# A streaming-encoder layer: the order of feed-forward pieces and block products behind the first part

## The chip, the core and the metric

The kernel runs on one core of a Trainium2 chip. The time is that of one execution on the device, in microseconds; before the change it is 1093.76 us, the median of three runs (1093.75 to 1093.88). Weights and activations are float32. TensorE (PE) multiplies, ScalarE (ACT) and VectorE (DVE) prepare its operands and work on its results, SyncE (SP) and GpSimd (POOL) issue transfers.

## What is computed

One layer: attention in two groups of heads, then a feed-forward with a causal convolution. The change touches the feed-forward alone:

```python
def conv_ffn(h, w_up_l, conv_w_l, conv_b_l, w_down_l):
    u = h @ w_up_l                                   # 256 x 2048 @ 2048 x 11264
    u = causal depthwise convolution of width 3 (u) + conv_b_l
    gate, val = jnp.split(u, 2, axis=-1)             # 5632 features each
    return (jax.nn.silu(gate) * val) @ w_down_l      # @ 5632 x 2048
```

There are 256 tokens, 2048 model columns and 5632 hidden features: 44 feature tiles of 128.

## The kernel before

**High and low.** A float32 weight tile `w_raw` is split in two: `w_hi` is a cast by ACT to the format that PE multiplies (L263), and `w_lo = w_raw - w_hi` is a subtraction by DVE (L271). PE multiplies `w_hi` with both parts of the activations (512 columns: high and low side by side) and `w_lo` with their high part alone (256 columns). `w_hi` and `w_lo` have three buffers each, taken in turn, `w_raw` has five. So the cast for one step takes the buffer of the step three before it, and waits until PE has done that step's products with `w_hi`.

**Parts and pieces.** The 44 feature tiles are cut into five parts of eight tiles and a last part of four (`FFN_PARTS`). Inside a part the tiles go in pairs; a pair is done for the gate and then for the value. The products of a pair with `w_up` need 16 blocks of rows, in two pieces of eight (`up_pieces`, `kh` 0 and 1), each one step: 16 products with `w_hi`, 16 with `w_lo`, all into one accumulator `pu`. A part of eight tiles has 16 such steps. When a pair's second piece is done, `convolved` brings the result through the convolution: ACT copies one half (L1061), DVE adds and scales (L1062, L1064), ACT makes the three taps (L1071, L1078), DVE adds them (L1083). The gate goes through SiLU on ACT (L1089); the value is multiplied with it by DVE (L1097) and split again into high and low, `g2` (L1100, L1102). After the last pair of a part, DVE and ACT also make sums of its tiles (L1111 to L1125), called `s`.

**Block products.** The multiplication with `w_down` works on the part before: `down_in_seven` computes a 2 x 2 block product with seven products of four blocks, one step each, with 8 products with `w_hi` and 4 with `w_lo`, all 512 columns wide. Their weights are loaded, or made by adding: a DVE sum of two raw tiles (L1233), or a transfer by POOL that adds into a raw tile (L1206). DVE adds each result to the output rows `xb` (L1175). A part has 14 such steps, for two halves of the output columns; they are dealt out among the up steps of the next part. The last part of four tiles has seven among its 8 up steps, and seven more after them, mixed with the plain pieces of its own `w_down` product (`down_plain`, accumulator `acc`).

**What sets the order.** All steps stand in one list. For each step in turn the kernel issues: what follows from earlier steps (the stages of `convolved`, in turn), the cast and subtraction for the step two ahead (`SPLIT`), the load for the step six ahead (`LOAD`), the DVE sum for the step four ahead (`SUM`), and the products of the step itself. PE, DVE, ACT and SP keep this order; each is a queue in which an instruction that waits holds up all behind it.

In part 0, which has no block products among its pieces, the second piece of a pair (but the last pair) does its products with `w_lo` first: `lows` is (1, 0) there, so that low follows low and high follows high between the pieces.

Of the kernel before, what the change touches and what calls it, by code (L numbers as in the profile page):

```python
# [45 lines left out]
def hybrid_layer(  # L46
# [173 lines left out]
    steps, following, after, waiting, running, others = [], [], [], deque(), [], []  # L220
# [5 lines left out]
    def new_step(load, sums, prepare, matmuls, follow=None, first=False):  # L226
        steps.append((load, sums, prepare, matmuls, follow, first))
# [12 lines left out]
    def acc_tile(name):  # L240
        nonlocal psa
        if psa is None:
            psu_ctx.close()
            psa = ctx.enter_context(
                tc.tile_pool(name="psa", bufs=1, space=bass.MemoryType.PSUM, side="right", reuse_waits="tile")
            )
        turn[0] ^= 1
        return psa.tile([P, 2, 512], F32, name=name, tag=f"acc{turn[0]}")
# [4 lines left out]
    def load(src, raw=None):  # L253
        if raw is None:
            raw = wraw.tile([P, 2048], F32, name="w_raw", tag="w_raw")
        a, b = src.shape[1:]
        nc.sync.dma_start(raw[:, : a * b].rearrange("p (a b) -> p a b", a=a), src)
        return raw
# [7 lines left out]
    def split(raw, a, b):  # L266
        return subtracted(raw, *cast(raw, a * b, act.copy), a, b)
# [9 lines left out]
    def rows_of(w, k0, n, c0, cols):  # L277
        return w[k0 * P : (k0 + n) * P, c0 : c0 + cols].rearrange("(k p) c -> p k c", p=P)
# [848 lines left out]
    def up_pieces(part, f0, follows):  # L1127

        c0 = f0 * P + (DFF if follows is val_follows else 0)
        cell, at_step = [], []  # L1130

        def piece(kh):
            mem = {}
            at_step.append(len(steps))
            lows = (1, 0) if kh and part.f_lo == 0 and f0 < part.f_hi - 2 and at_step[1] == at_step[0] + 1 else (0, 1)

            def loads():
                mem["raw"] = load(rows_of(wu, 8 * kh, 8, c0, 2 * P))

            def prepare():  # L1140
                mem["parts"] = split(mem["raw"], 8, 2 * P)

            def matmuls():
                if kh == 0:
                    cell.append(acc_tile("pu"))
                acc, (hi, lo) = cell[0], mem["parts"]
                first = kh and part.f_lo == f0 == 0 and follows is gate_follows
                halves = (range(4), range(4, 8)) if first else (range(8),)
                order = (0, 1) if first else lows
                for ks, low, j in [(ks, low, j) for ks in halves for low in order for j in range(2)]:  # L1150
                        for i in ks:
                            k = 8 * kh + i
                            nc.tensor.matmul(  # L1153
                                acc[:, j, S:] if low else acc[:, j, :],
                                (lo if low else hi)[:, i, j * P : (j + 1) * P],
                                hT[:, k, 0, :] if low else hT[:, k].rearrange("p a b -> p (a b)"),
                                start=k == 0 and not low, stop=k == KT - 1 and low == order[1],
                            )

            new_step(loads, None, prepare, matmuls, (lambda: follows(part, cell[0], f0)) if kh else None)  # L1160

        piece(0)
        yield
        piece(1)
        yield

# [122 lines left out]
    for f_lo, f_hi in FFN_PARTS:  # L1289
        part = Part(f_lo, f_hi)  # L1290
        pieces = [
            p for f in range(f_lo, f_hi, 2) for follows in (gate_follows, val_follows)
            for p in [up_pieces(part, f, follows)] * 2
        ]
        if last is None:
            behind = []
        elif f_hi < NFT:
            behind = [g for c in (0, 1024) for g in [down_in_seven(last, c)] * 7]
        else:
            second = down_in_seven(last, 1024)  # L1300
            behind = [down_in_seven(last, 0)] * 7
        behind = deque(behind)
        at_piece = range(len(pieces) - len(behind), len(pieces))
        for i, piece in enumerate(pieces):
            next(piece)
            if i in at_piece:
                next(behind.popleft())
        if f_hi < NFT:
            last = part
# [109 lines left out]
```

## Time and profile before

| | |
|---|---|
| time, median of three runs | 1093.76 us (1093.75 to 1093.88) |
| profiled execution, first to last instruction | 1091.8 us |
| what the median has around that span | 1.96 us |
| PE busy | 1087.3 us |
| DVE busy | 924.2 us |
| ACT busy | 755.1 us |
| feed-forward, from the first product of its first up step | from 384.2 us on |

The page groups instructions by line, engine and tile; the views used below also list instructions in order of time, as "start, length, engine, line, operation, out<-in, shape, count", with the idle time before and what ended it in brackets. PE's rows overlap a little, since matmuls are pipelined: the distance between the starts of two rows is the time that the first one takes of PE.

### The profile page before, as it was taken

To read this page: it belongs to the slowest core of one execution; us is meant where nothing else is said; L and a number is where in the kernel's file an instruction comes from. 1 tells how busy PE (TensorE), PEld (TensorE's weight loads), DVE (VectorE), ACT (ScalarE), POOL (GpSimd) and SP (SyncE) were. 2 spreads that over 40 slices of the span, in tenths; PEclk is the share of its full clock that TensorE was granted. 3 is DMA by queue.
4 is the path that set the end of the run, shared out by engine and by line. 5 is a ranking of instruction groups with operands and counts; after the bars stand their busy time and mean duration, and the time that the engine had idled before them with its cause. 6 is when DMAs were issued, how large, how long until landed. Compare 5 with 4: busy or idle time off the path is not lost.

```text
span 1091.8 us, 14685 instructions
## 1 busy us (share of the span) xinstructions
PE 1087.3 (100%) x5701; PEld 939.5 (86%) x5701; DVE 924.2 (85%) x918; ACT 755.1 (69%) x968; POOL 59.0 (5%) x53
## 2 busy tenths in 40 slices
PE   9999999999999999999999999999999999999998
PEld 9988888888888888888888888888888888888887
DVE  5988899888897667779887988889898889879996
ACT  6767697767766657767766776677667767667763
POOL 0000000001000000000000000100000000000000
PEclk9999999999999999999999999999999999999999
DMA  8897886868777465669989597996969799896995
GB/s 310 276 272 239 271 206 196 253 183 271 239 214 251 154 199 161 214 170 249 288 206 316 173 265 254 254 296 170 302 195 271 241 246 279 215 319 161 291 247 155
DMA packets 175215, 258.53 MB, mean 237 GB/s; under 512 B 4632, under 2 KB 98218, under 8 KB 175146
## 3 DMA queue, kind: packets, MB, share of 16 engines
q1 hardware_dynamic: 151690, 210.26, 56.9%
q0 software_dynamic: 23280, 47.19, 24.5%
q8 instruction: 45, 0.74, 0.3%
q14 instruction: 24, 0.20, 0.1%
q10 hardware_dynamic: 176, 0.14, 0.0%
HBM read 255.48 MB, written 2.10 MB: 236 GB/s over the span
## 4 chain that ended last, share of the span: by engine, by line
PE 100%; DVE 0%; issue 0%
PE pu L1153 45%; PE bank_a L291 18%; PE bank_b L291 11%; PE bank_c L291 6%; PE acc_o L291 6%; PE acc_v L411 4%; PE bank_e L291 2%; PE acc L291 2%; PE ps_x L192 1%; PE ps_h L637 1%; PE ps_o L709 1%; PE ps_z L785 0%; PE ps_o L710 0%; PE ps_z L805 0%; PE ps_i L186 0%; PE half L291 0%
## 5 line engine op out<-in xcount | busy, mean ns | idle before, releaser
L271 DVE TENSOR_TENSOR w_lo<-w_raw,w_hi 128x2048 fp32r<-128x2048 f32 (+2 forms) x251 | 555.9, 2219 | 124.1 <-ACT w_hi L263 123.1
L263 ACT CAST w_hi<-w_raw 128x2048 fp32r<-128x2048 f32 (+2 forms) x251 | 464.6, 1854 | 220.7 <-PE pu L1153 90.0
L1153 PE MATMUL pu<-hT,w_hi 128*128 128x512 f32 x1408 | 333.6, 390 | 0.0
L1153 PEld LDWEIGHTS pu<-hT,w_hi 128*128 128x128 f32 x1408 | 263.1, 188 | 53.6
L1153 PEld LDWEIGHTS pu<-hT,w_lo 128*128 128x128 f32 x1408 | 180.0, 191 | 6.5
L1153 PE MATMUL pu<-hT,w_lo 128*128 128x256 f32 x1408 | 182.1, 283 | 0.0
L1206 POOL DMA_DIRECT2D w_raw<-in_w_down_dram x31 | 39.8, 1302 | 715.9 <-DVE w_lo L271 384.7
L1078 ACT ACTIVATE tap<-up,ccol 128x256 f32<-128x256 f32 x176 | 74.6, 495 | 0.0
L291 PE MATMUL bank_a<-w_hi,hT 128*128 128x512 f32 x192 | 48.5, 395 | 0.0
L291 PEld LDWEIGHTS bank_a<-w_hi,hT 128*128 128x128 f32 x192 | 35.2, 188 | 6.7
L291 PE MATMUL bank_b<-w_hi,s 128*128 128x512 f32 x160 | 40.1, 393 | 0.0
L291 PE MATMUL bank_a<-w_hi,s 128*128 128x512 f32 x160 | 40.0, 392 | 0.0
L291 PE MATMUL bank_a<-w_hi,g 128*128 128x512 f32 x152 | 38.0, 392 | 0.0
L411 PE MATMUL acc_v<-w_hi,hT 128*128 128x344 f32 x192 | 35.7, 328 | 0.0
L291 PEld LDWEIGHTS bank_b<-w_hi,s 128*128 128x128 f32 x160 | 28.8, 189 | 5.5 <-issue 0.3
L291 PEld LDWEIGHTS bank_a<-w_hi,s 128*128 128x128 f32 x160 | 28.9, 189 | 5.2
L1083 DVE TENSOR_TENSOR gate<-gate,tap 128x512 f32<-128x512 f32 x44 | 30.3, 689 | 2.7 <-DVE gate L1083 0.5
L1083 DVE TENSOR_TENSOR val<-val,tap 128x512 f32<-128x512 f32 x44 | 30.3, 689 | 2.3
L291 PE MATMUL acc_o<-w_hi,oSb 128*128 128x512 f32 x128 | 31.8, 397 | 0.0
L1064 DVE TENSOR_TENSOR up<-t,R 128x512 f32<-128x512 f32 x44 | 30.5, 692 | 1.5
L291 PEld LDWEIGHTS bank_a<-w_hi,g 128*128 128x128 f32 x152 | 27.4, 189 | 4.9
L411 PEld LDWEIGHTS acc_v<-w_hi,hT 128*128 128x128 f32 x192 | 30.4, 190 | 0.5 <-DVE hT L203 0.2
(293 smaller groups left out, 1411.2 us busy)
## 6 DMA issues: line engine op xcount, KB each, us to landing
w_raw<-in_w_up_dram SPq DMA_DIRECT2D x88, 1024.0 KB, 7.0
w_raw<-in_w_down_dram SPq DMA_DIRECT2D x44, 1024.0 KB, 6.7
w_raw<-in_w_in_dram SPq DMA_DIRECT2D x40, 1024.0 KB, 5.5
w_raw<-in_w_down_dram POOLq DMA_DIRECT2D x31, 1024.0 KB, 9.8
w_raw<-in_w_out_dram SPq DMA_DIRECT2D x16, 1024.0 KB, 7.7
w_raw<-in_w_in_dram POOLq DMA_DIRECT2D x10, 1024.0 KB, 9.4
w_raw<-in_w_in_dram SPq DMA_DIRECT2D x13, 516.0 KB, 5.5
xb<-in_x_dram POOLq DMA_DIRECT2D x4, 512.0 KB, 8.7
```

Of the source, the lines that this page charges most:

```text
L192: nc.tensor.transpose(ps[:, j, t * P : (t + 1) * P], x2[:, t, (k + j) * P : (k + j + 1) * P], ident)
L263: copy(hi[:, :n], raw[:, :n])
L271: dve.tensor_tensor(lo[:, :n], raw[:, :n], f32(hi[:, :n]), op=ALU.subtract)
L291: nc.tensor.matmul(o, lhs(i, l, t), r[:, i, :] if cut is None else r[:, i, cut], start=starts and j == 0, stop=stops and j == 3 * n - 1, s ...
L411: nc.tensor.matmul(banks[j][t][:, :VC], of_half(hT[:, k], l, t), w[:, 0, m * VC : (m + 1) * VC], start=k == l == 0 and w is mem["parts", i ...
L637: nc.tensor.transpose(ps[:, h, :], rows[n, t][:, h * HD : (h + 1) * HD], ident)
L709: mm(po, v, w[:, i, :S], start=m == 0, stop=False)
L1064: dve.tensor_tensor(u[:, :, 2:], t2, R, op=ALU.mult)
L1078: act.activation(taps[w][:, j, :], u[:, j, w : w + S], AF.Copy, scale=ccol[:, w, f : f + 1])
L1083: dve.tensor_tensor(a, a, tap, op=ALU.add)
L1153: nc.tensor.matmul(acc[:, j, S:] if low else acc[:, j, :], (lo if low else hi)[:, i, j * P : (j + 1) * P], hT[:, k, 0, :] if low else hT[: ...
L1206: nc.gpsimd.dma_start(mem[weights].rearrange("p (a b) -> p a b", a=4), plus, accum_op=ALU.add)
```

## The change

```diff
@@ up_pieces
-        cell, at_step = [], []
+        cell = []
 
         def piece(kh):
             mem = {}
-            at_step.append(len(steps))
-            lows = (1, 0) if kh and part.f_lo == 0 and f0 < part.f_hi - 2 and at_step[1] == at_step[0] + 1 else (0, 1)
+            lows = (1, 0) if kh and (part.f_lo or f0 < part.f_hi - 2) else (0, 1)
@@ the loop over the parts
         at_piece = range(len(pieces) - len(behind), len(pieces))
         for i, piece in enumerate(pieces):
             next(piece)
-            if i in at_piece:
+            for _ in {i - 1, i}.intersection(at_piece) if i % 2 else ():
                 next(behind.popleft())
```

In every part behind the first, the block products no longer follow each up step but come two at a time behind each pair; the first two pairs of a part are followed by no product and by two, and in the last part by one and by two. The second piece of every pair there now does its products with `w_lo` first. What is multiplied, loaded and added stays the same. Lines below L1134 move up by one.

On PE, where the second group of products of part 1 stands (`pu` is an up step, `bank_b` a block product). Before:

```order
L1153 MATMUL pu<-hT,w_hi 128x512 x16
L1153 MATMUL pu<-hT,w_lo 128x256 x16
L291 MATMUL bank_b<-w_hi,s 128x512 x8
L291 MATMUL bank_b<-w_lo,s 128x512 x4
L1153 MATMUL pu<-hT,w_hi 128x512 x16
L1153 MATMUL pu<-hT,w_lo 128x256 x16
```

Now:

```order
L1152 MATMUL pu<-hT,w_hi 128x512 x16
L1152 MATMUL pu<-hT,w_lo 128x256 x32
L1152 MATMUL pu<-hT,w_hi 128x512 x16
L291 MATMUL bank_b<-w_hi,s 128x512 x8
L291 MATMUL bank_b<-w_lo,s 128x512 x4
```

Two up steps stand in a row, with all 32 products with `w_lo` between those with `w_hi`, and two products (the second has rows like the first) behind them.

On PE, at the start of part 1, with the numbers of the tiles. Before:

```order
L1153 MATMUL pu_4237<-hT_94,w_hi_4131 128x512 x16
L1153 MATMUL pu_4237<-hT_94,w_lo_4132 128x256 x16
L1153 MATMUL pu_4237<-hT_94,w_hi_4177 128x512 x16
L1153 MATMUL pu_4237<-hT_94,w_lo_4178 128x256 x16
L1153 MATMUL pu_4333<-hT_94,w_hi_4226 128x512 x16
```

Now:

```order
L1152 MATMUL pu_4237<-hT_94,w_hi_4131 128x512 x16
L1152 MATMUL pu_4237<-hT_94,w_lo_4132 128x256 x16
L1152 MATMUL pu_4237<-hT_94,w_lo_4178 128x256 x16
L1152 MATMUL pu_4237<-hT_94,w_hi_4177 128x512 x16
L1152 MATMUL pu_4333<-hT_94,w_hi_4226 128x512 x16
```

The part's second up step ends with `w_hi_4177`, where it ended with `w_lo_4178`.

On DVE, at the end of the last part, from the subtraction for the seventh block product on. Before:

```order
L271 TENSOR_TENSOR w_lo<-w_raw,w_hi 128x2048
L1175 TENSOR_TENSOR xb<-xb,bank_a 128x512
L271 TENSOR_TENSOR w_lo<-w_raw,w_hi 128x2048
L1233 TENSOR_TENSOR w_raw<-w_raw 128x2048
L271 TENSOR_TENSOR w_lo<-w_raw,w_hi 128x2048
L1062 TENSOR_TENSOR t_8911<-pu,t_8911 128x512
L1064 TENSOR_TENSOR up_3440<-t_8911,R_90 128x2x256
L1175 TENSOR_TENSOR xb<-xb,bank_a 128x512
L271 TENSOR_TENSOR w_lo<-w_raw,w_hi 128x2048
L1083 TENSOR_TENSOR val<-val,tap 128x512 x2
L1097 TENSOR_TENSOR gate<-gate,val 128x512
```

Now (the first row holds the subtractions for the sixth and seventh product and for the first of the last seven):

```order
L271 TENSOR_TENSOR w_lo<-w_raw,w_hi 128x2048 x3
L1062 TENSOR_TENSOR t_8891<-pu,t_8891 128x512
L1064 TENSOR_TENSOR up_3440<-t_8891,R_90 128x2x256
L1232 TENSOR_TENSOR w_raw<-w_raw 128x2048
L1174 TENSOR_TENSOR xb<-xb,bank_a 128x512
L271 TENSOR_TENSOR w_lo<-w_raw,w_hi 128x2048
L1083 TENSOR_TENSOR val<-val,tap 128x512 x2
L1097 TENSOR_TENSOR gate<-gate,val 128x512
L1174 TENSOR_TENSOR xb<-xb,bank_a 128x512
L271 TENSOR_TENSOR w_lo<-w_raw,w_hi 128x2048
L1102 TENSOR_TENSOR g_8946<-gate,g_8946 128x512
```

The convolution of the last pair (L1062, L1064) and the sum of raw tiles (L1232) now stand ahead of the subtraction for the second of the last seven products, and the taps ahead of the third.

## The prediction

> **What bounds the kernel now.** I read the page first, then the waits, then the order of time on each engine at three places of the feed-forward.
>
> ```profile
> span 1091.8 us, 14685 instructions
> PE 1087.3 (100%) x5701; PEld 939.5 (86%) x5701; DVE 924.2 (85%) x918; ACT 755.1 (69%) x968; POOL 59.0 (5%) x53
> PEclk9999999999999999999999999999999999999999
> PE 100%; DVE 0%; issue 0%
> ACT w_hi L263 <- PE pu L1153: 90.0, 42, 3.0
> ```
>
> PE (TensorE) is busy throughout, the chain that ended last lies on it alone, and its clock was granted in full. So there are two ways to change the time: matmuls that take less room one behind the other, or PE waiting, which it does not do now. VectorE (DVE) has 15% to spare on average, but an average says nothing about one stretch. The last row shows who sets ACT's pace: the cast that makes `w_hi` waits for PE to finish the step three earlier, whose buffer it takes (three buffers of `w_hi`, three of `w_lo`).
>
> Names: U0, U1, ... are the up steps of a part (an odd one is the second piece of its pair), P0 to P6 the seven products put between them, S0 to S6 the last seven products, A0 the first plain piece between S2 and S3. "Highs" are the products with `w_hi`, "lows" those with `w_lo`.
>
> **What the change saves.** Part 0 already runs its pairs as all later ones now shall, so its rows give the price.
>
> ```profile
> 404.49 7.45 PE L1153 MATMUL pu<-hT,w_hi 128*128 128x512 f32 x32
> 448.94 7.44 PE L1153 MATMUL pu<-hT,w_hi 128*128 128x512 f32 x32
> 456.22 2.08 PE L1153 MATMUL pu<-hT,w_lo 128*128 128x256 f32 x16
> 489.62 2.08 PE L1153 MATMUL pu<-hT,w_lo 128*128 128x256 f32 x16
> ```
>
> From 404.49 to 448.94 lie four pairs of the merged form (32 highs, 32 lows): 44.45 / 4 = 11.112 us each. From 456.22 to 489.62 lie six steps in the form high, low, high, low: 33.40 / 6 = 5.567, so 11.133 a pair. A merged pair saves 0.021 us. It holds for 8 pairs in each of parts 1 to 4 and 4 in part 5: 36 x 0.021 = **0.75 us saved**. Two products side by side save nothing beyond that: their matmuls are as wide as the highs.
>
> **What it costs: the buffer that comes free late.** A second piece with its lows first finishes its highs last, so its `w_hi` is released about 1.9 us later than now. And where two products follow a pair, a cast must wait for that pair's end, with 5.4 us of PE work, not 8.3, to cover it and what follows. Three places are tight.
>
> *Start of part 1.* In the new order U1's highs end with the step, at 485.97, and not at 484.06, where its lows begin today.
>
> ```profile
> 484.06 2.08 PE L1153 MATMUL pu<-hT,w_lo 128*128 128x256 f32 x16
> 484.26 1.91 ACT L263 CAST w_hi<-w_raw 128x2048 fp32r<-128x2048 f32 x1 [1.07 <-PE pu L1153]
> 486.23 2.29 DVE L271 TENSOR_TENSOR w_lo<-w_raw,w_hi 128x2048 fp32r<-128x2048 f32 x1 [1.15 <-ACT w_hi L263]
> 485.97 3.82 PE L1153 MATMUL pu<-hT,w_hi 128*128 128x512 f32 x16
> 493.80 2.28 DVE L271 TENSOR_TENSOR w_lo<-w_raw,w_hi 128x2048 fp32r<-128x2048 f32 x1
> 496.00 2.49 DVE L1125 TENSOR_TENSOR s<-gate,s 128x512 fp32r<-128x512 f32 x4
> 496.72 1.09 ACT L1071 ACTIVATE gate<-up,ccol 128x256 f32<-128x256 f32 x2 [2.19 <-DVE s L1125]
> 497.72 1.70 ACT L1078 ACTIVATE tap<-up,ccol 128x256 f32<-128x256 f32 x4
> 499.32 1.90 ACT L263 CAST w_hi<-w_raw 128x2048 fp32r<-128x2048 f32 x1
> 501.25 4.62 DVE L271 TENSOR_TENSOR w_lo<-w_raw,w_hi 128x2048 fp32r<-128x2048 f32 x2 [0.76 <-ACT w_hi L263]
> 502.57 3.79 PE L1153 MATMUL pu<-hT,w_hi 128*128 128x512 f32 x16
> ```
>
> The cast at 484.26 takes U1's buffer. PE to ACT takes 0.2 us (484.06 to 484.26), so it moves to 486.17: 1.91 later. From 486.23 on DVE has no gap until 498.4 (convolution, the sums of products, the four `s`), ACT's `gate` at 496.72 waits for `s`, and the cast at 499.32 stands behind the taps. All of it moves by 1.91: that cast, U4's, ends at 503.13. U4 starts at about 502.55 in both orders (the same steps lie ahead): **0.7 us** of waiting, with 0.1 for the hand-over. Then DVE still has, in a row, the subtraction of U4 (2.2), two operations of the convolution (1.33), an addition (0.6) and U5's subtraction (2.29), from 503.2: it ends at 509.6. U5 starts with its lows, at 503.25 + 5.55 = 508.8: **0.9 us** more.
>
> *Start of parts 2 to 4.* From U3's end, T: U4's cast starts at T + 0.2 at best (U3's buffer) and at T + 0.55 where the taps ahead of it are late, and ends 1.9 later. DVE then does U4's subtraction, 1.33 of convolution, the sum of two raw tiles (2.2, no such step in part 1), an addition and U5's subtraction: 0.55 + 1.97 + 2.2 + 1.33 + 2.2 + 0.6 + 2.29 = 11.1. U5's lows are due at T + 5.44 + 5.55 = 11.0. I take **0.2 us** for each of the three; from none to 0.6, by when the taps end.
>
> *The end of part 5.* Here P5, P6, S0, S1, S2 are five products in a row, 2.72 us each.
>
> ```profile
> 1038.29 1.90 ACT L263 CAST w_hi<-w_raw 128x2048 fp32r<-128x2048 f32 x1
> 1040.70 2.29 DVE L271 TENSOR_TENSOR w_lo<-w_raw,w_hi 128x2048 fp32r<-128x2048 f32 x1
> 1043.02 2.29 DVE L1233 TENSOR_TENSOR w_raw<-w_raw 128x2048 f32<-128x2048 f32 x1
> 1045.23 2.29 DVE L271 TENSOR_TENSOR w_lo<-w_raw,w_hi 128x2048 fp32r<-128x2048 f32 x1
> 1047.43 0.68 DVE L1062 TENSOR_TENSOR t<-pu,t 128x512 f32<-128x512 f32 x1
> 1048.15 0.69 DVE L1064 TENSOR_TENSOR up<-t,R 128x512 f32<-128x512 f32 x1
> 1048.76 0.68 DVE L1175 TENSOR_TENSOR xb<-xb,bank_a 128x512 f32<-128x512 f32 x1
> 1049.35 2.28 DVE L271 TENSOR_TENSOR w_lo<-w_raw,w_hi 128x2048 fp32r<-128x2048 f32 x1
> 1051.56 1.48 DVE L1083 TENSOR_TENSOR val<-val,tap 128x512 f32<-128x512 f32 x2
> 1053.07 0.69 DVE L1097 TENSOR_TENSOR gate<-gate,val 128x512 f32<-128x512 f32 x1
> 1054.28 2.28 DVE L271 TENSOR_TENSOR w_lo<-w_raw,w_hi 128x2048 fp32r<-128x2048 f32 x1
> 1056.48 0.69 DVE L1102 TENSOR_TENSOR g<-gate,g 128x512 fp32r<-128x512 f32 x1
> 1047.02 1.98 PE L291 MATMUL bank_a<-w_hi,g 128*128 128x512 f32 x8
> 1049.74 1.98 PE L291 MATMUL bank_c<-w_hi,g 128*128 128x512 f32 x8
> 1051.56 1.07 PE L291 MATMUL bank_c<-w_lo,g 128*128 128x512 f32 x4
> ```
>
> Today S0's cast runs at 1038.29, before U7 (the last up step) has even started, since it takes P5's buffer. DVE works without a gap from there, and S1's `w_lo` (1045.23 + 2.29 = 1047.52) is ready 4.0 us before its lows at 1051.56; S2's (1051.63) 2.7 us before its own (1049.74 + 2.72 + 1.82 = 1054.28); A0's (1056.56) 0.4 before 1057.0. In the new order S0's cast takes U7's buffer and must wait for X, the end of U7. From X, with steps as the rows are spaced: cast 0.2 + 1.97 = 2.17; S0's subtraction 2.2, t and up 1.33, the sum 2.2, an addition 0.6, S1's subtraction 2.29: 10.8, with the hand-over 10.86. S1's lows are due after P5, P6, S0 and S1's highs: 3 x 2.72 + 1.82 = 9.98. **0.9 us.** Then taps 1.5, product 0.6, addition 0.6, S2's subtraction 2.29: 15.85, due at 10.86 + 0.9 + 1.82 = 13.6. **2.2 us.** Then `g` 0.6, addition 0.6, A0's subtraction 2.29: 19.25, due at 15.85 + 0.9 + 1.82 = 18.55. **0.7 us.** A0 (two products' length, 5.44) gives DVE room again. So 3.8 in all.
>
> **Sum.** 0.7 + 0.9 + 3 x 0.2 + 3.8 = 6.0 us of waiting, less 0.75: **+5.25 us**, a span of 1097.05. The median of the runs (1093.76) lies 1.96 over the profiled span; with the same around it, **1099.0 us**. The hand-over from DVE or ACT to PE is not seen, as PE never waits; from ACT to DVE it is 0.03 us (499.32 + 1.90 to 501.25), from PE to ACT about 0.2. I took 0.07 to 0.1, near the first; with either end the eight waits change by -0.4 to +0.8. At other places the same sums leave room (0.5 us at part 5's U3 and U5, over 2 us in the steady pairs), so they cost nothing while transfers land as now.
>
> The clock was granted in full in all 40 slices, with no gap in PE's work to try it. [...]
>
> **Rivals.**
>
> *Not slower: the waits are hidden.* If U7's late release did not hold S0's cast, or DVE had a store of finished tiles, only the 0.75 us would be left: 1093.0. For it: PE waits nowhere now, and even S1's `w_lo` is 4.0 us early. Against it: that lead is the third buffer, and the late release takes just that; it needs DVE to be 4 us ahead at U7's end, while the rows show it working without a gap to 1057. It decides where S1's subtraction ends under X + 9.98. Chance 0.12.
>
> *The end alone.* The start of part 1 has room that I do not see (DVE in another order of arrival, an earlier `s`), and parts 2 to 4 lose nothing: 3.8 - 0.75 = +3.05, 1096.8. Chance 0.13.
>
> *Late transfers on top.*
>
> ```profile
> w_raw<-in_w_down_dram POOLq DMA_DIRECT2D x31, 1024.0 KB, 9.8
> ```
>
> The adding transfers from POOL take 9.8 us, and P6's follows P4's subtraction, which follows P4's transfer: two in a chain. P6's cast has 2.7 us before S0's; where each lands 2.2 us later, the end loses 1.7 us more: 1100.7. Two loads now also follow each other for P0, P1 and P2, P3, but with four loads per four steps as before. Chance 0.14.
>
> *Faster by more than 0.2%* would take 2.2 us, three times what the switches cost. No row speaks for it. Chance 0.03.
>
> **How the numbers follow.** My forecast has 0.58, the rivals 0.12, 0.13, 0.14, 0.03. About 0.2% (2.2 us) is what this measurement tells from no change. Slower by more: 0.58 + 0.13 + 0.14 = 0.85; within: 0.12; faster: 0.03. The range goes from below the end-alone case to above the late transfers: 1096.2 to 1101.2.
>
> **What would show it.** In the new profile PE should have idle time before `bank_c` and `bank_b` at the end (0.9 and 2.2), before `acc` (0.7), and before U4 and U5 of part 1 (0.7, 0.9), each ended by DVE's `w_lo` or ACT's `w_hi`; the merged pairs should last 11.11 us. I am wrong if PE stays at 100% with a span near 1091, if S0's cast starts before U7 ends, or if the waits end with a DMA.

## The result, and the profile after

The changed kernel takes **1168.33 us**, the median of five runs (1166.5 to 1168.6), against 1093.88 us for the kernel before on the same chip: 1.0676 times, with a 95% interval of 1.0664 to 1.0688. Slower was forecast, but by 5.25 us; it is 74.5 us. The profiled execution spans 1166.5 us, 74.7 more than before. From the page of the changed kernel:

```profile
span 1166.5 us, 14670 instructions
PE 1111.3 (95%) x5701; PEld 953.5 (82%) x5701; DVE 926.5 (79%) x918; ACT 751.6 (64%) x968; POOL 58.9 (5%) x53
PE 86%; issue 5%; DVE 5%; ACT 3%; DMA 1%; DVEq 0%; ACTq 0%
```

The work is the same (5701 matmuls), yet PE no longer sets the end by itself: the chain of waits now runs over DVE and ACT too. PE is busy 24 us longer with the same matmuls, and idle for about 50 us besides. The view of waits says what PE waited for (total, times, longest):

```profile
PE bank_a L291 <- DVE xb L1174: 34.8, 9, 5.8
PE bank_b L291 <- DVE xb L1174: 14.7, 4, 3.7
PE pu L1152 <- DVE w_lo L271: 0.6, 1, 0.6
PE pu L1152 <- ACT w_hi L263: 0.5, 1, 0.5
```

The last two are the waits that the prediction put at U5 and U4 of part 1. The first two, 13 waits, stand nowhere in it. One of them, in order of time (part 1; P4 and P5, both `bank_a`, behind the pair U6, U7):

```profile
538.41 1.98 PE L291 MATMUL bank_a<-w_hi,s 128*128 128x512 f32 x8
538.61 1.91 ACT L263 CAST w_hi<-w_raw 128x2048 fp32r<-128x2048 f32 x1 [5.58 <-PE pu L1152]
540.22 1.07 PE L291 MATMUL bank_a<-w_lo,s 128*128 128x512 f32 x4
540.55 2.29 DVE L271 TENSOR_TENSOR w_lo<-w_raw,w_hi 128x2048 fp32r<-128x2048 f32 x1 [5.17 <-ACT w_hi L263]
542.76 0.68 DVE L1062 TENSOR_TENSOR t<-pu,t 128x512 f32<-128x512 f32 x1
543.48 0.69 DVE L1064 TENSOR_TENSOR up<-t,R 128x512 f32<-128x512 f32 x1
544.09 0.68 DVE L1174 TENSOR_TENSOR xb<-xb,bank_a 128x512 f32<-128x512 f32 x1
544.92 3.39 PE L291 MATMUL bank_a<-w_hi,s 128*128 128x512 f32 x8 [3.63 <-DVE xb L1174]
548.14 1.09 PE L291 MATMUL bank_a<-w_lo,s 128*128 128x512 f32 x4
```

P4's last matmul makes room at 540.22 + 4 x 0.227 = 541.13. P5 adds to the bank that P4 has just filled, so it must not begin before DVE has added P4's result to `xb` (544.09, done at 544.77). It begins at 544.92: a **stop of 3.79 us** (the bracket says 3.63, since it counts from the modelled end of the matmul before). DVE was late because of the row ahead of that addition, a subtraction whose cast waited for the end of the pair at 538.41, and two rows of the convolution, which need the same end.

Behind the stop there is a second loss. P5's first eight matmuls last 3.39 us where P4's took 1.98. The windows of PE's time show it (one row each: the stretch, its length, PE busy, PEld, DVE, ACT, POOL, granted clock, transfer share, GB/s):

```profile
537.40:540.80 3.40, 3.40 (x17) 2.81 (x16) 0.24 (x1) 2.19 (x2) 0.00 (x0) 1.00 1.11 251
540.80:544.20 3.40, 0.49 (x3) 0.07 (x1) 3.37 (x4) 2.00 (x2) 0.00 (x0) 1.00 0.69 223
544.20:547.60 3.40, 2.68 (x6) 2.16 (x7) 2.77 (x2) 2.69 (x6) 0.00 (x0) 0.52 0.87 298
547.60:551.00 3.40, 3.40 (x16) 2.79 (x15) 1.29 (x2) 1.92 (x1) 0.00 (x0) 0.98 0.75 261
```

After a stretch in which PE was nearly idle (0.49 of 3.40 us), the clock was granted at 0.52 for 3.4 us, and then at 0.98. It fell behind all 13 stops: over the first 2.4 us of the product behind, it was 0.50 at ten of them and 0.76 to 0.78 at three (from 665.96, 809.23 and 952.57).

The whole: 13 stops, 49.5 us in the view of waits and 0.16 more each by the starts of the matmuls, **51.6 us**; each of the 13 products behind them lasts 4.1 to 5.25 us instead of 2.72, **21.1 us**; the two waits in part 1 with the slower first matmuls behind them 1.5; less 0.75 for the merged pairs. That is 73.5 of the 74.7. Of the last 1.2 us, 0.8 are the ends of three slow stretches that reach into the next up step (its first matmuls, at 670.14, 813.33 and 956.68, are 0.43 us and not 0.227 apart), and 0.2 lie ahead of the feed-forward (first up step at 384.42, before at 384.22).

### The profile page after: what moved, and what is told of

Read it like the earlier page. It is cut to its first block, busy times and chain, and to the rows that moved or that the text cites. A ratio compares the mean times of both kernels' runs of the same rounds, so it can differ in the third digit from the quotient of the medians.

```text
span 1166.5 us, 14670 instructions
## 1 busy us (share of the span) xinstructions
PE 1111.3 (95%) x5701; PEld 953.5 (82%) x5701; DVE 926.5 (79%) x918; ACT 751.6 (64%) x968; POOL 58.9 (5%) x53
## 4 chain that ended last, share of the span: by engine, by line
PE 86%; issue 5%; DVE 5%; ACT 3%; DMA 1%; DVEq 0%; ACTq 0%
PE pu L1152 40%; PE bank_a L291 15%; PE bank_b L291 9%; PE bank_c L291 5%; PE acc_o L291 4%; PE acc_v L411 4%; ACT w_hi L263 3%; PE bank_e L291 2%; PE acc L291 2%; DVE w_lo L271 1%; DVE t L1062 1%; DVE xb L1174 1%; DMA w_raw<-in_w_out_dram 1%; PE ps_x L192 1%; PE ps_h L637 0%
## 5 line engine op out<-in xcount | busy, mean ns | idle before, releaser
L1152 PEld LDWEIGHTS pu<-hT,w_lo 128*128 128x128 f32 x1408 | 175.3, 192 | 4.6 <-DVE w_lo L271 0.8
L1152 PE MATMUL pu<-hT,w_lo 128*128 128x256 f32 x1408 | 176.7, 283 | 0.6 <-DVE w_lo L271 0.6
L291 PE MATMUL bank_a<-w_hi,g 128*128 128x512 f32 x152 | 45.6, 451 | 20.3 <-DVE xb L1174 20.3
L291 PE MATMUL bank_a<-w_hi,s 128*128 128x512 f32 x160 | 45.6, 434 | 14.5 <-DVE xb L1174 14.5
L291 PEld LDWEIGHTS bank_a<-w_hi,g 128*128 128x128 f32 x152 | 33.5, 224 | 29.5 <-issue 16.1
L291 PE MATMUL bank_b<-w_hi,s 128*128 128x512 f32 x160 | 43.2, 416 | 14.7 <-DVE xb L1174 14.7
L291 PEld LDWEIGHTS bank_a<-w_hi,s 128*128 128x128 f32 x160 | 34.0, 215 | 23.3 <-issue 16.1
L1071 ACT ACTIVATE val<-up,ccol 128x256 f32<-128x256 f32 x44 | 24.1, 594 | 23.3 <-DVE up L1064 23.2
L1071 ACT ACTIVATE gate<-up,ccol 128x256 f32<-128x256 f32 x44 | 24.1, 595 | 19.5 <-DVE up L1064 16.9
L1174 DVE TENSOR_TENSOR xb<-xb,bank_a 128x512 f32<-128x512 f32 x40 | 27.2, 682 | 7.4 <-PE bank_a L291 7.3
```

The source lines that it names most:

```text
L291: nc.tensor.matmul(o, lhs(i, l, t), r[:, i, :] if cut is None else r[:, i, cut], start=starts and j == 0, stop=stops and j == 3 * n - 1, s ...
L1071: act.activation(a[:, j, :], u[:, j, 2:], AF.Identity, scale=ccol[:, 2, f : f + 1], bias=ccol[:, 3, f : f + 1],)
L1152: nc.tensor.matmul(acc[:, j, S:] if low else acc[:, j, :], (lo if low else hi)[:, i, j * P : (j + 1) * P], hT[:, k, 0, :] if low else hT[: ...
L1174: dve.tensor_tensor(xs, xs, ps[h // 256][:, :n] if last_one else ps[:, h : h + n], op=op)
```

## The experiments

**Its own bank for each product.** Is it the shared bank?

```diff
-                if new:
+                if True:
                     mem[bank] = psb.tile([P, 512], F32, name=bank, tag="t")
-                in_three([mem[bank]], mem["parts", bank, to], 4, lhs(), new, True)
+                in_three([mem[bank]], mem["parts", bank, to], 4, lhs(), True, True)
```

> The change with one thing taken away: each of the seven products gets a PSUM bank of its own and starts it anew, so the second of two products no longer adds to a bank that DVE must first have read. Left out: products are no longer added on to the product before them in the same bank, so the output rows lack those terms; matmuls, casts, subtractions, transfers and additions to the output are as many as in the change. Theory A (PE waits because the second product of a bank stands right behind the first, and DVE's addition lies between them): the 13 waits (9 before bank_a, 4 before bank_b) are gone, and what is left is the sum of the prediction, 6.0 us of other waits less 0.75: 1097 to 1099 us, with waits at the start of part 1 (0.5 and 0.6), at S1, S2 (0.9, 2.2) and A0 (0.7). Rival B (the loss comes from the late buffers of the lows-first order, of which DVE's addition is only the last link): the waits move to other matmuls and the time stays over 1150 us.

Measured: 1100.57 us, 1.0060 times the kernel before (1.0045 to 1.0075). All 13 stops are gone, and what PE waits for is the list of the prediction, without A0:

```profile
PE bank_b L291 <- DVE w_lo L271: 1.9, 1, 1.9
PE pu L1152 <- DVE w_lo L271: 1.1, 4, 0.6
PE bank_c L291 <- DVE w_lo L271: 0.7, 1, 0.7
PE pu L1152 <- ACT w_hi L263: 0.5, 1, 0.5
```

Theory A holds. It is 1.6 us over A's upper end, because the clock fell once here too, behind the 1.9:

```profile
1053.70:1057.10 3.40, 2.71 (x12) 1.94 (x11) 3.26 (x5) 0.77 (x2) 0.18 (x1) 1.00 0.73 111
1057.10:1060.50 3.40, 1.51 (x7) 0.91 (x6) 3.40 (x4) 3.40 (x3) 0.56 (x1) 0.99 1.11 230
1060.50:1063.90 3.40, 3.40 (x9) 2.64 (x8) 3.40 (x4) 0.69 (x2) 0.72 (x1) 0.51 1.08 330
```

**The two halves of the change.** Products in twos, highs first as before:

```diff
-            lows = (1, 0) if kh and (part.f_lo or f0 < part.f_hi - 2) else (0, 1)
+            lows = (1, 0) if kh and part.f_lo == 0 and f0 < part.f_hi - 2 else (0, 1)
```

> Half of the change: block products two at a time behind each pair, while each piece behind part 0 keeps its highs first and its lows last, as before the change. Theory A: the same 13 places wait, but each about 1.9 us less, since the cast on which DVE's queue hangs may start 1.9 us earlier: 11 waits of about 1.8 us, one of 3.2 (part 1's first), one of 4.0 (the last), 27 us in all. [...] Rival B (the lows-first order alone makes the loss): 1094 to 1096 us.

Measured: 1124.89 us, 1.0286 times (1.0270 to 1.0301). The same 13 places wait, but less:

```profile
PE bank_a L291 <- DVE xb L1174: 17.6, 9, 3.9
PE bank_b L291 <- DVE xb L1174: 8.3, 4, 3.1
```

Eleven stops are 1.87 to 1.90 us long, 1.92 shorter than in the change, as the cast may start 1.91 us earlier. Part 1's first is 3.25, the last 4.07. The clock fell behind the last alone (its eight highs took 3.29 us), not behind the 3.25 (1.00, and 2.08 us): the loss is 28.0 us of stops and 3.0 of slower or restarted matmuls.

Lows first, products dealt one behind each up step as before:

```diff
-            for _ in {i - 1, i}.intersection(at_piece) if i % 2 else ():
+            if i in at_piece:
                 next(behind.popleft())
```

> The other half of the change: the second piece of each pair behind part 0 does its lows first, and the block products stay one behind each up step, as before the change. Theory A: no two products of one bank stand side by side, so none of the 13 waits is there; what is left are waits for casts and subtractions that start later, 5.4 us by the rows of the kernel before (0.7 and 0.6 at the start of part 1, 3.0 at the last part's end, 1.1 around the first plain piece): 1099 us. Rival B (the lows-first order alone makes the loss): over 1150 us.

Measured: 1103.47 us, 1.0092 times (1.0074 to 1.0109). None of the 13 stops is there; rival B falls. The forecast 0.7, 0.6, 3.0 and 1.1 are there as 0.60, 0.35, 3.08 and 0.85 us. One wait was not forecast, in part 4:

```profile
831.33 1.91 ACT L263 CAST w_hi<-w_raw 128x2048 fp32r<-128x2048 f32 x1 [6.82 <-DMA w_raw<-in_w_up_dram]
835.61 3.63 PE L1152 MATMUL pu<-hT,w_lo 128*128 128x256 f32 x16 [2.53 <-DVE w_lo L271]
```

A load landed late, the cast waited for it, PE stopped for 2.69 us, and the clock fell behind that (0.51 from 835.90 to 839.30). This kernel's runs also spread most (1102.0 to 1106.7). Why the load was late stays open.

The halves cost 31.0 and 9.6 us alone, 74.5 together: the late buffer makes twelve of the 13 stops 1.9 us longer (part 1's first 0.6), and with that the clock fell behind every one (0.50 to 0.78, as above), where with highs first it fell behind one.

**Idle matmuls in the stops.** Is the slowness behind a stop a matter of the gap? (`beside` says that the step ahead is a product of the same bank; the dots mark lines left out.)

```diff
+            beside = mem.get(("at", bank)) == len(steps) - 1
+            mem["at", bank] = len(steps)
 ...
+                if beside:
+                    for i in range(16):
+                        nc.tensor.matmul(mem["bank_c"], hT[:, 0, 0, :P], hT[:, i].rearrange("p a b -> p (a b)"), start=True, stop=True)
                 if new:
```

> The change, and at each of the 13 places where the second product of a bank stands right behind the first, 16 more matmuls of 512 columns between them (3.63 us by the pitch of 0.227 us), whose results go to a bank that is free there and are used by nobody. They take the place of the wait, so PE has no gap there. Theory A with the clock: the wait was lost anyway, so the fill costs nothing, but without a gap the matmuls behind it run at full speed (5.25 us becomes 2.72): the 13 places lose 3.8 us each (the last 5.9), 52 us in all, and the time is about 1146 us, 22 us below the change. Rival C (the matmuls behind the wait are slow for another reason, such as DVE reading the bank or the subtraction beside it): the time stays at 1168 us. Rival D (it is not a wait at all but work that PE must do): 1168 + 13 x 3.63 = 1215 us.

Measured: 1149.59 us, 1.0510 times (1.0492 to 1.0527), 18.7 us below the change, with 208 matmuls more. The product behind the fill is back at its old length:

```profile
538.60 3.79 PE L1223 MATMUL bank_c<-hT 128*128 128x512 f32 x16
542.39 2.09 PE L291 MATMUL bank_a<-w_hi,s 128*128 128x512 f32 x8
544.31 1.07 PE L291 MATMUL bank_a<-w_lo,s 128*128 128x512 f32 x4
```

So C and D fall. The median is 3.6 us above A's figure. The profiled execution's span, 1145.7, is 53.9 over before, where A gave 52. A filled stop is as long as the wait was: from 538.60 to 542.39 are 3.79 us, 3.63 of matmuls and 0.16 of waiting, and all 13 together are 51.6 us as in the change. What A left out are the two waits in part 1 (1.5), a first matmul 0.11 us slower behind each of the 13 (1.4), and the saving (0.75); with them it is 53.9. The profiled execution was the fastest of the four (1147.65 to 1149.83), and the rest lies in their spread.

**How long a gap may be.** The same with 8 and with 4 idle matmuls (`range(8)`, `range(4)`), each timed once:

> The change with 8 idle matmuls (1.81 us) between the two products of a bank at the 13 places, so that gaps of about 2.0 us are left (the last 4.2). Wait and fill together last as long as the wait of the change. [...] Rival P (any gap that is there at all slows the matmuls behind it): 13 x 1.4 us more than with no gap: 1166 us.

> The change with 4 idle matmuls (0.91 us) at the 13 places, which leaves gaps of about 2.9 us (the last 5.1). [...]

Measured: 1156.91 and 1165.97 us. With gaps of 2.0 us, 4 of the 12 have slow matmuls behind them; with 2.9 us, 11 of 12; and in both the last, longer one. Rival P, by which every gap slows the matmuls behind it, falls. One slow and one undisturbed gap of the run with 8:

```profile
519.71:523.13 3.42, 1.56 (x7) 1.00 (x6) 3.39 (x5) 2.02 (x4) 0.00 (x0) 0.99 1.12 212
523.13:526.54 3.41, 3.41 (x9) 2.67 (x8) 1.51 (x1) 1.95 (x5) 0.00 (x0) 0.51 1.08 337
540.20:543.61 3.41, 2.63 (x12) 1.85 (x10) 3.30 (x3) 2.34 (x3) 0.00 (x0) 1.00 0.71 249
543.61:547.02 3.41, 2.38 (x11) 1.99 (x12) 3.09 (x3) 2.91 (x7) 0.00 (x0) 1.00 0.94 306
```

Behind the gap from 520.57 to 522.59, 2.02 us, the clock was 0.51 and the eight highs took 3.36 us. Behind the gap from 542.67 to 544.64, 1.97 us, it stayed at 1.00.

**The addition put ahead.** How much of a stop is due to the bank, and how much to DVE's order?

```diff
         advance(following)
+        if n in early:
+            at_step(0, 3)
+            begun = steps[n][4]()
+            next(begun)
         at_step(SPLIT, 2)
```

(`early` holds the first of two products of one bank that stand side by side; the lines that fill it are left out here. The step's products are then not issued again further down.)

> The change, and at the 13 places DVE's addition of the first product is put ahead of the subtraction and the convolution steps that stand before it in DVE's order; the products stay side by side and add to one bank as in the change. Theory A (the wait of 3.8 us is made by what stands ahead of the addition on DVE, and only 0.9 us of it, the hand-overs and the addition's 0.6, are due to the bank itself): 13 waits of about 0.9 to 1.0 us, ended by the same addition, and no slow matmuls behind them; with the other waits of the prediction (0.5, 0.6 at the start of part 1; 0.7 to 2.1 at S1, S2, A0) 17.6 us in all, less 0.75, plus 1 to 3 for restarts and one stretch of slow clock at the end: 1111 to 1114 us. Rival B (a second product of a bank waits some 3.8 us whatever stands ahead of the addition, for instance for the hand-over through PSUM): about 1168 us.

Measured: 1114.23 us, 1.0184 times (1.0167 to 1.0201), 0.2 us above the upper end of theory A.

```profile
536.60 0.69 DVE L1174 TENSOR_TENSOR xb<-xb,bank_a 128x512 f32<-128x512 f32 x1 [4.30 <-PE bank_a L291]
537.21 2.28 DVE L271 TENSOR_TENSOR w_lo<-w_raw,w_hi 128x2048 fp32r<-128x2048 f32 x1
537.43 2.09 PE L291 MATMUL bank_a<-w_hi,s 128*128 128x512 f32 x8 [0.87 <-DVE xb L1174]
```

The addition now starts 0.2 us behind P4's place and PE stops for 1.03, 13 times, with no slow matmul behind any (the eight highs above took 2.09 us). One more stop at such an addition, 0.98 us at 1098.24, is new: it stands before the sixth of the last seven products. So of each 3.79 us, 1.03 belong to the shared bank (addition and two hand-overs), and 2.76 to what stood ahead of the addition on DVE.

**Banks of their own and highs first.** The first experiment's edit with that of the second:

> Products two at a time, highs first as before the change, and a PSUM bank of its own for each product, which it starts anew. Left out, as before: a product no longer adds to the one before it in its bank. Theory A: neither the 13 waits nor the waits by late buffers at the starts of the parts; by the rows of the kernel before only 1.1 us at S2 and 0.7 at A0 remain, since the end of part 5 still has five products in a row: 1095.6 us, up to 1097 if the clock falls once. Against the run with banks of their own and lows first (1100.6) the difference of some 4 to 5 us is what the lows-first order costs. Rival B: as that run, 1100 us or more.

Measured: 1096.17 us, 1.0019 times (1.0009 to 1.0028): the 4.4 us to the first experiment is what the lows-first order costs once the stops are away; what is left are 1.2 us at S2 and 0.4 at A0, behind five products in a row.

**The change without its collisions.** The question left is whether the merged form is worth anything. (The dots mark lines left out; the first case of `deal` keeps the order of the kernel before.)

```diff
-            lows = (1, 0) if kh and (part.f_lo or f0 < part.f_hi - 2) else (0, 1)
+            lows = (1, 0) if kh and part.f_hi < NFT and part.f_lo != FFN_PARTS[1][0] and f0 < part.f_hi - 2 else (0, 1)
 ...
+        if last is None or f_hi == NFT or f_lo == FFN_PARTS[1][0]:
+            deal = [int(i in at_piece) for i in range(len(pieces))]
+        else:
+            deal = [0, 1, 0, 2, 0, 2, 0, 1, 0, 2, 0, 2, 0, 2, 1, 1]
         for i, piece in enumerate(pieces):
             next(piece)
-            for _ in {i - 1, i}.intersection(at_piece) if i % 2 else ():
+            for _ in range(deal[i]):
                 next(behind.popleft())
```

> The change without its collisions: in parts 2 to 4 the products come in groups of 1, 2, 2, 1, 2, 2, 2 behind seven pairs (P0; P1 P2; P3 P4; P5; P6 and the next P0; P1 P2; P3 P4), then P5 between the two pieces of the last pair and P6 behind it, so that no two products that add to one bank stand side by side; the seven whole pairs do their lows in the middle. Part 1, part 5 and the end stay as before the change. Theory A (the collisions are the loss, and the merged form is worth 0.021 us a pair): PE waits nowhere, 21 x 0.021 = 0.44 us saved: 1093.4 us, between 1093.2 and 1094.0. Rival B (products in twos or the late buffers cost by themselves): the three parts bring their share of the loss, over 1096 us.

Measured: 1093.53 us, 0.9997 times (0.9988 to 1.0005): no difference that this measurement can tell. (Six pairs a part were merged, not seven: the seventh belongs to the last two feature tiles, whose pairs I had left as they were. The saving to look for was 18 x 0.021 = 0.38 us.) No stop at a product in those parts (one of 0.2 us stands at 1061.55, in the end that was not changed), so B falls; a version that clearly beats the kernel before was not found.

## Why the prediction was wrong

**The step that failed** is the sentence "Two products side by side save nothing beyond that: their matmuls are as wide as the highs", and with it the sum of costs, which looked only for waits on `w_hi` and `w_lo`. I costed two products side by side by their matmuls alone and never asked what the second waits for. P3 adds to P2's bank, P5 and P6 to P4's; `product("bank_b", False, ...)` says so in the code. The rows of the kernel before show what was covered:

```profile
508.11 2.00 PE L291 MATMUL bank_b<-w_hi,s 128*128 128x512 f32 x8
510.86 3.79 PE L1153 MATMUL pu<-hT,w_hi 128*128 128x512 f32 x16
514.25 0.68 DVE L1175 TENSOR_TENSOR xb<-xb,bank_b 128x512 f32<-128x512 f32 x1
516.40 2.00 PE L291 MATMUL bank_b<-w_hi,s 128*128 128x512 f32 x8
```

P2 ends at 510.86, its addition at 514.93, P3 begins at 516.40. The addition is 4.1 us behind its product, hidden by the 5.55 us of the up step between them. That step was the cover, and the change moved it away.

The 4.1 us are not the price, though. At the 13 places the addition ends between 0.89 and 4.07 us behind its product in the kernel before, 24.8 us in all; that 13 x 4.07, some 53 us, comes near the measured 51.6 is luck. The shortest one, at the last collision of part 1, with nothing ahead of the addition:

```profile
592.82 1.07 PE L291 MATMUL bank_a<-w_lo,s 128*128 128x512 f32 x4
593.92 0.69 DVE L1175 TENSOR_TENSOR xb<-xb,bank_a 128x512 f32<-128x512 f32 x1 [0.38 <-PE bank_a L291]
```

The price comes from what the new order puts ahead of the addition on DVE. From the end of the pair (538.41 in the rows of the result) to P5 run the cast (0.2 + 1.91), the subtraction (2.2), two rows of the convolution (1.33), the addition (0.68) and the hand-overs, 6.51 us together; P4 covers 2.72 of them, and 3.79 are bare. These are the terms of which the prediction built its sum for S1; it asked only when the next `w_lo` would be ready.

The runs show what the shared bank cost here: with a different bank 13 stops are gone (1100.57 us), with the same one each cost at least 1.03 us, even with the addition put ahead.

**The clock** is the second part. The sum has no term for it, and the kernel before, with a mean granted clock of 0.999, gave none. In the run with banks of their own the clock was 0.51 behind a stop of 2.05 us (1.89 in the view of waits), and in the change some 19 us hang on it, by what the 16 idle matmuls gave back (18.7).

**Point by point**, the rest:

| step | forecast | measured (waits as in the view of waits) |
|---|---|---|
| U4 of part 1 | 0.7 | 0.47 in the change |
| U5 of part 1 | 0.9 | 0.62 in the change |
| U5 of parts 2 to 4 | 0.2 each | 0.16 each, with banks of their own |
| S1 | 0.9 | 0.69, with banks of their own |
| S2 | 2.2 | 1.89, with banks of their own |
| A0 | 0.7 | none there, but its highs took 3.34 us, at a granted clock of 0.51, and not 1.98 |
| a group of two up steps and two products | 0.021 less | 16.55 us, from 16.57 |

The last row is the way from one group to the next: 704.30 to 720.87 before, 565.64 to 582.19 in the change. So nearly every term of the sum was there, somewhat smaller than forecast; by the starts of the matmuls each wait is 0.06 to 0.16 us longer than in the view, and so nearer to it. (The last of the sums, 15.85 + 0.6 + 0.6 + 2.29, is 19.34 and not 19.25, which would make A0's 0.7 a 0.8.) With banks of their own they bring 1100.6 us, the clock's fall included, against the 1099.0 of the sum. In the changed kernel itself the waits of parts 2 to 4 and of the end are absent: there the stops give DVE time to catch up. The last stop, 5.99 us before P6, comes two steps ahead of S1. With the short stops of the run in which the addition is put ahead, the waits at S1, S2 and A0 are back (0.30, 1.91 and 0.38).

**The rivals.** None had the cause. "The waits are hidden" and "the end alone" were wrong in the size of the whole; "late transfers on top" shows in no wait of the changed kernel, but once in the run with the lows-first order alone.

## What to carry to other kernels

When work is moved away from between two instructions, list what it had covered: not only the operands that the next instruction reads, but also the place that it writes to, who still reads that, and what stands ahead of that reader on its engine. For a matmul that goes on adding to a bank, add up, in the new order, what stands ahead of that bank's read-out on its engine, from the moment that the first of it can start; what the work left between does not cover is a stop: here there was one at each of the 13 places (at P5 of part 1, 6.51 us less the 2.72 that P4 covered: 3.79). How late the read-out is in the trace of before says only where to look: here it was 0.9 to 4.1 us, and the new order changed it. And a stop on PE can cost more than its length: in the run with 8 idle matmuls the product behind a gap of 2.02 us took 4.42 us and not 2.72, while with highs first the products behind stops of 1.87 to 1.90 us took 2.82 to 2.84.

## What the hardware showed

The granted clock fell to 0.5 for stretches of about 3.4 us: it was 0.51 from 1060.50 to 1063.90 with banks of their own and from 523.13 to 526.54 with 8 idle matmuls (both above). At the first and the last stop of the change it stayed at 0.50 for about twice as long. At the last it was 0.50 in each microsecond from 1114.40 to 1120.40 (PE began work again at 1117.35), and 1.00 from 1121.40 on. The rows of the first (PE was idle for almost half of the one stretch and busy through the other):

```profile
520.43:523.84 3.41, 1.81 (x4) 1.50 (x5) 3.38 (x4) 2.52 (x6) 0.00 (x0) 0.50 1.10 238
523.84:527.25 3.41, 3.41 (x9) 2.67 (x8) 0.25 (x1) 1.56 (x2) 0.00 (x0) 0.50 1.09 367
```

In these runs the length of a stop alone did not say whether the clock fell behind it. A stop of 3.25 us with highs first had no slow matmul behind it (granted clock 1.00); one of 2.05 us (the 1.89 above with the hand-over) had (0.51). In the run with 8 idle matmuls, gaps of about 2.0 us had slow matmuls behind them four times in twelve (2.02 us had, 1.97 us had not, above). In the run with 4, gaps of 2.9 us had them eleven times in twelve (behind one the eight highs took 3.47 us); the twelfth, from 540.91 to 543.79, had not. With highs first, stops of 1.87 to 1.90 us had no slow matmul behind them, eleven times. One of them, from 1003.98 to 1005.85, with eight highs in 2.08 us behind it:

```profile
1002.46:1005.87 3.41, 1.70 (x9) 1.11 (x7) 3.38 (x5) 2.60 (x3) 0.00 (x0) 1.00 0.47 90
1005.87:1009.28 3.41, 3.41 (x15) 2.84 (x16) 3.31 (x3) 3.24 (x6) 0.00 (x0) 1.00 0.84 290
```

What decides which stops have slow matmuls behind them was not shown.
